# Three start-up stretches of a hybrid encoder layer in another order: filter-tap folds in attention, five products of MLP block 1 among the last norms, the second MLP product's first loads on ScalarE's queue

## The chip, the cores and the metric

The kernel runs on one core of one Trainium2 chip. The metric is the device time of one execution in microseconds (us), lower is better; a run's time is a little longer than the span between its first and last instruction in the trace.

## What is computed

One encoder layer in fp32 for 2048 tokens of width 1024. Cut to what matters here:

```python
a = rms_norm(h, norm1_g)
q, k, v, u = split(a @ w_in)              # 512, 128, 128, 1536 columns
att = block_attention(rope(norm(q)), rope(norm(k)), v)   # 8 heads of 64, 2 key/value heads
hy = hyena_mixer(u, ...)                  # short convolution, two long filters by FFT
mix = concat([rms_norm(att, attn_out_g), rms_norm(hy, hy_out_g)])
h = h + mix @ w_out                       # 1024 x 1024
m = rms_norm(h, norm2_g)
h = h + square(relu(m @ w_mlp_in)) @ w_mlp_out   # 1024 -> 4096 -> 1024
return rms_norm(h, final_g)
```

## The kernel before

Every fp32 product is split into high and low fp32r parts and done as three matmuls (`mm3`, lines 162 to 166: high by high, high by low, low by high). So a left operand is made in two steps: ScalarE casts the high part, VectorE subtracts to get the low part. The stages follow each other: input projection, attention (1238 us at its end) with the projection of u and the filter taps woven in, the transform of the filters and the convolutions, `mix` (the output projection with norm, 1770 to 1895 us), `mlp_in` (to 2525 us) and `mlp_out` (from 2541 us).

**Attention.** A unit of work is 128 queries and one key/value head. Its scores go to TensorE (`peak`, L461; VectorE takes the maxima, L464), then 16 steps of exponentials on ScalarE (L484). GpSimd adds the 16 exponential tiles into `sum` (L489), then `os` (L494), ScalarE copies the weighted values beside it (L505), and GpSimd adds the two halves to `ob` (L507), from which TensorE makes `of` (L513). GpSimd works through its instructions strictly in order. Towards the end of attention the generator `taps_ahead` opens a `Feed`: it loads tiles `x` of the filter taps from memory (L1381, on SP's queue) and folds each into `e` with one addition and one subtraction (L1398, L1399). The engines take turns by `FOLD = gps, vec, gps, gps`; five folds are made ahead, and a tile scheduler, not a hand-written order, decides where they stand between the sums.

**The mix and MLP block 1.** Both MLP products use seven products of half-size operands in place of eight (Strassen's scheme). `mix` walks over 16 token tiles (iteration n = 0 to 15). Per tile: `added` and `squared` (residual, sum of squares), `normed` (m), `turned` (eight transposes into `mt` on TensorE, L776), `taken` (ScalarE copies `mt` with the gain into `sa` or `sb`, L790). Tiles come in pairs; after the second, four subtractions (L802) make the operands of the seven products, and `keep` stores them to `mo_d` by DMAs that GpSimd issues (L799). `sb` has one buffer, so the copies of a tile into it wait until the stores of the pair before have landed. This part is written in program order for TensorE, VectorE, ScalarE and GpSimd (`in_order`). The generator `mlp_in` is stepped from within by `next(mlp)`: it loads blocks of `w_mlp_in` as `w1raw`, and `prepare` makes a left operand `wop` (ScalarE L914, VectorE L915). For product 6, 7, 5 or 3 of a block it first needs the sums `ws` of quarter blocks (`left_sums`, L705 to L708: VectorE in block 0 of the loop, GpSimd later). Those `ws` lie in the pool `mi`, which takes the memory of the pool `mx` of the mix, and is opened only after it. Products are written (block, p); `seq` runs (0,1), (0,2), (0,6), (0,7), (0,5), (1,1), (1,2), (0,3), (1,6) ... by `CYCLE`. Before, (0,1) and (0,2) are made while the last tiles are normed, and everything else after the mix is through.

**The second MLP product.** `mlp_out` runs over steps (p, f). A step loads 512 KB of hidden values `ar` from `H_d` and 256 KB of weights `x`, splits both (`ah` L1090 and L1112, `bh` L1082) and makes 24 matmuls `y`. The first `OLOAD = 3` steps are loaded ahead: the first on ScalarE's queue, the others on SP's, in whose queue the last stores of `H_d` stand before them. Their tiles lie where `mlp_in` had its own, so a load can wait for what was there.

Of the kernel before, what the change touches and what calls it, by code (L numbers as in the profile page):

```python
# [20 lines left out]
P = 128  # L21
# [423 lines left out]
def attention(k, a1, ps, side):  # L445
# [12 lines left out]
    def peak(u, i):  # L458
        b, h = i // G, i % G
        s = ps.get("sc", "sc")  # L460
        nc.tensor.matmul(s[:], u.q[:, h], kt[u.kv, b][0][:], start=True, stop=True)  # L461
        if i == 0:
            u.top = a1.tile([P, G, 4], F32, name="top", bufs=2)
        nc.vector.tensor_reduce(out=u.top[:, h, b:b + 1], in_=s[:], axis=AX.X, op=ALU.max, negate=True)  # L464
        if i == 15:
            low = a1.tile([P, 16], F32, name="low", bufs=2)[:, :G]
            nc.vector.tensor_reduce(out=low, in_=u.top[:], axis=AX.X, op=ALU.min)
            u.diag = a1.tile([P, G, P], F32R, name="diag", bufs=2)
            nc.vector.tensor_mul(out=u.diag[:], in0=k.ident[:].unsqueeze(1).to_broadcast([P, G, P]),
                                 in1=low.unsqueeze(2).to_broadcast([P, G, P]))  # L470
# [6 lines left out]
    def weights(u, j):  # L477
# [10 lines left out]
        elif j < 15:  # L488
            nc.gpsimd.tensor_add(out=u.sum[:], in0=u.p0[:] if j == 1 else u.sum[:], in1=p[:])  # L489
# [228 lines left out]
M_SLOT = {1: 0, 2: 1, 3: 3, 4: 6, 5: 4, 6: 5, 7: 2}  # L718


def mix(k, mo, pool, ps, wo, mlp):
# [5 lines left out]
    k.mh, k.ml = ([mo.tile([P, 4, 4, P], F32R, name=f"m{part}{i}", bufs=1) for i in range(7)] for part in "hl")  # L727
# [28 lines left out]
    def room(u):  # L756
        u.m = mo.tile([P, DM], F32, name="m", tag="raw", bufs=NRAW)
        u.ssq = pool.tile([P, 1], F32, name="r2s", bufs=2)
# [20 lines left out]
    def taken(u):  # L779
# [3 lines left out]
        if s == 0:  # L783
            k.sa = pool.tile([P, 2, 4, P], F32, name="sa", bufs=2)
        else:
            k.sb = pool.tile([P, 5, 4, P], F32, name="sb", bufs=1)
# [4 lines left out]
        if s:  # L791
            op = [k.sa[:, 0], k.sa[:, 1]] + [k.sb[:, j] for j in range(5)]
            b11, b21, b12, b22, t1, t2, t4 = op
            engine = nc.gpsimd if half and i == 3 else nc.vector

# [5 lines left out]
            def sub(out, in0, in1, *js):  # L801
                engine.tensor_sub(out=out, in0=in0, in1=in1)  # L802
# [29 lines left out]
    for n in range(NT):  # L832
# [34 lines left out]
        if n % 2 == 0:  # L867
            add_up(5)
# [4 lines left out]
    for j in range(2):  # L873
        added(old, j)
    squared(old)
    normed(old)
    taken(older)
    add_up(99)
    turned(old)
    taken(old)  # L880
# [6 lines left out]
def mlp_in(k, mo, ps):  # L887
# [3 lines left out]
    raws, sums, ops, blk = {}, {}, {}, {}  # L891
    k.mi = None

# [7 lines left out]

    def prepare(n, p):
# [5 lines left out]
        if p == 6:  # L908
            t = [k.mi.tile([P, 4, P], F32, name=f"ws{i}", bufs=1 + (i == 3))[:] for i in range(4)]
            q = sums[n][0]  # L910
            left_sums(nc.gpsimd if n else nc.vector, *t, q["11"], q["12"], q["21"], q["22"])
            sums[n].update({3: t[3], 5: t[0], 6: t[1], 7: t[2]})
# [14 lines left out]
    def tile(name, bufs):  # L927
        return k.mi.tile([P, 512], F32, name=name, bufs=bufs)
# [34 lines left out]
    for x in seq[:2]:  # L963
        prepare(*x)
        early.append(product(*x))
    yield
    for x in seq[2:LEAD]:
        prepare(*x)
    for i, (n, p) in enumerate(seq):
# [4 lines left out]
        b, g = blk[n], early[i] if i < 2 else product(n, p)  # L974
# [41 lines left out]
def mlp_out(k, pool, ps):  # L1016
# [31 lines left out]
    for name, new in ("wr", raw_w), ("ah", parts_h):  # L1048
# [3 lines left out]
    for name, new in ("x", kept), ("bh", parts_w), ("ar", raw_h):  # L1052
        held[name] = [new()]
# [6 lines left out]
    def load(i):  # L1060
        p, f = steps[i]
        queue = nc.sync if i else nc.scalar
# [95 lines left out]
    nc.sync.dma_start(out=k.gf[:], in_=a["final_g"].unsqueeze(0).to_broadcast([P, DM]))  # L1158
    for i, (p, f) in enumerate(steps):
        if i + OLOAD < len(steps):  # L1160
# [279 lines left out]
def taps_ahead(k, ps):  # L1440
# [4 lines left out]
    yield  # L1445
    yield
    for _ in range(FEED_F[1] - 1):
        k.feed.fold_next()
# [305 lines left out]
def encoder_layer(tc, a):  # L1754
    with ExitStack() as ctx:
# [10 lines left out]
        with sbuf(k, "wa") as k.wa:  # L1766
            with Banks(k, "ps3", {"s": 4}, {"x": 2}) as ps:
# [9 lines left out]
                with sbuf(k, "mo") as mo:  # L1777
                    mlp = mlp_in(k, mo, ps)
                    with sbuf(k, "mx") as mx, in_order(tc):
                        mix(k, mo, mx, ps, k.wo1, mlp)  # L1780
# [22 lines left out]
```

## Time and profile before

| | us |
|---|---|
| median of three runs | 3157.62 |
| lowest, highest | 3154.59, 3162.08 |
| the profiled execution | 3165.88 |
| its span in the trace | 3164.1 |
| TensorE busy in it | 2989.5 |

Read it with TensorE in mind: the span is TensorE's busy time and what lies between. A row of an engine in order of time gives the start, the duration, the instruction, and in brackets the idle time before it with what ended that. A matmul of 512 columns shows 0.39 us at the full clock of 2.4 GHz and 0.63 us at 1.2 GHz, since the rows overlap; matmuls follow each other at 0.23 and 0.43 us.

### The profile page before, as it was taken

To read this page: it belongs to the slowest core of one execution; us is meant where nothing else is said; L and a number is where in the kernel's file an instruction comes from. 1 tells how busy PE (TensorE), PEld (TensorE's weight loads), DVE (VectorE), ACT (ScalarE), POOL (GpSimd) and SP (SyncE) were. 2 spreads that over 40 slices of the span, in tenths; PEclk is the share of its full clock that TensorE was granted. 3 is DMA by queue.
4 is the path that set the end of the run, shared out by engine and by line. 5 is a ranking of instruction groups with operands and counts; after the bars stand their busy time and mean duration, and the time that the engine had idled before them with its cause. 6 is when DMAs were issued, how large, how long until landed. Compare 5 with 4: busy or idle time off the path is not lost.

```text
span 3164.1 us, 40514 instructions
## 1 busy us (share of the span) xinstructions
PE 2989.5 (94%) x13400; PEld 2251.3 (71%) x13400; DVE 2048.8 (65%) x3153; ACT 1423.2 (45%) x2626; POOL 1715.1 (54%) x1399
## 2 busy tenths in 40 slices
PE   8978999999998998999999988999999989999998
PEld 6755666666665666676667766888788778888887
DVE  7987777666665554777465567778877535454455
ACT  7866655555553444444444563333433223223333
POOL 3434777778776876244555326777876635250010
PEclk9988999999998999999999998999999999999999
DMA  7758334324334425776656784445644395333454
GB/s 226 221 155 232 115 125 159 110 95 151 125 107 108 140 80 163 263 248 218 186 172 197 253 290 157 156 154 174 204 158 151 121 316 171 133 115 129 146 181 153
DMA packets 482462, 534.45 MB, mean 169 GB/s; under 512 B 49604, under 2 KB 344004, under 8 KB 475212
## 3 DMA queue, kind: packets, MB, share of 16 engines
q1 hardware_dynamic: 464540, 513.16, 50.4%
q0 software_dynamic: 4480, 14.68, 1.3%
q10 hardware_dynamic: 13232, 4.01, 0.6%
q8 instruction: 107, 1.75, 0.2%
q14 instruction: 103, 0.84, 0.1%
HBM read 326.22 MB, written 198.19 MB: 166 GB/s over the span
## 4 chain that ended last, share of the span: by engine, by line
PE 75%; DVE 5%; DMA 5%; issue 3%; POOL 3%; ACT 2%; SPq 1%; ACTq 0%; POOLq 0%; DVEq 0%
PE o L502 7%; PE y L164 6%; PE y L165 6%; PE y L166 6%; PE g L166 5%; PE g L165 5%; PE g L164 5%; PE st L481 4%; PE X L1435 4%; PE st L482 3%; PE sc L461 3%; PE uo L164 3%; PE uo L165 2%; PE uo L166 2%; PE b L1565 2%
## 5 line engine op out<-in xcount | busy, mean ns | idle before, releaser
L489 POOL TENSOR_TENSOR sum<-sum,p 128x512 f32<-128x512 f32 x416 | 552.9, 1329 | 125.3 <-ACT p L484 98.9
L464 DVE TENSOR_REDUCE top<-sc 128x1 f32<-128x512 f32 x512 | 347.4, 687 | 255.4 <-PE sc L461 252.3
L484 ACT ACTIVATE p<-st 128x512 f32<-128x512 f32 x512 | 303.2, 597 | 317.6 <-PE st L482 299.9
L164 PE MATMUL g<-mh,wop 128*128 128x512 f32 x896 | 350.5, 391 | 17.9 <-ACT wop L914 17.6
L165 PE MATMUL g<-ml,wop 128*128 128x512 f32 x896 | 350.6, 391 | 2.8 <-DVE ml L925 2.8
L166 PE MATMUL g<-mh,wop 128*128 128x512 f32 x896 | 350.4, 391 | 2.4 <-DVE wop L915 2.4
L164 PE MATMUL y<-bh,ah 128*128 128x512 f32 x768 | 299.8, 391 | 15.5 <-ACT bh L1082 15.5
L1091 DVE TENSOR_TENSOR ah<-ar,ah 128x1024 fp32r<-128x1024 f32 x111 | 148.9, 1342 | 235.2 <-ACT ah L1090 232.9
L165 PE MATMUL y<-bh,ah 128*128 128x512 f32 x768 | 299.7, 390 | 0.0
L166 PE MATMUL y<-bh,ah 128*128 128x512 f32 x768 | 299.7, 390 | 0.0
L1090 ACT CAST ah<-ar 128x1024 fp32r<-128x1024 f32 x111 | 117.0, 1054 | 347.8 <-PE y L166 343.0
L502 PE MATMUL o<-p,vt 128*64 128x512 f32 x1024 | 234.9, 598 | 0.0
L461 PE MATMUL sc<-kt,q 128*128 128x512 f32 x512 | 208.0, 410 | 15.0 <-DVE top L464 11.9
L481 PE MATMUL st<-q,kt 128*128 128x512 f32 x512 | 215.0, 420 | 1.6 <-ACT p L484 1.4
L164 PEld LDWEIGHTS g<-mh,wop 128*128 128x128 f32 x896 | 169.2, 189 | 54.2 <-ACT wop L914 18.0
L482 PE MATMUL st<-q,kt 128*128 128x512 f32 x512 | 203.8, 398 | 0.0
L165 PEld LDWEIGHTS g<-ml,wop 128*128 128x128 f32 x896 | 169.0, 189 | 38.9 <-DVE ml L925 3.9
L166 PEld LDWEIGHTS g<-mh,wop 128*128 128x128 f32 x896 | 169.1, 189 | 38.4 <-DVE wop L915 3.5
L914 ACT CAST wop<-ws 128x512 fp32r<-128x512 f32 x128 | 79.1, 621 | 223.5 <-PE g L166 192.1
L164 PEld LDWEIGHTS y<-bh,ah 128*128 128x128 f32 x768 | 144.7, 189 | 46.2 <-ACT bh L1082 15.9
L166 PEld LDWEIGHTS y<-bh,ah 128*128 128x128 f32 x768 | 144.7, 188 | 30.3
L165 PEld LDWEIGHTS y<-bh,ah 128*128 128x128 f32 x768 | 144.7, 188 | 30.2 <-DVE bh L1083 0.2
(306 smaller groups left out, 7054.6 us busy)
## 6 DMA issues: line engine op xcount, KB each, us to landing
ar<-H_d SPq DMA_DIRECT2D x111, 512.0 KB, 3.8
uw<-uw_d SPq DMA_DIRECT2D x36, 1024.0 KB, 5.0
w1raw<-in_w_mlp_in SPq DMA_DIRECT2D x64, 512.0 KB, 4.2
H_d<-r SPq DMA_DIRECT2D x96, 256.0 KB, 2.2
H_d<-s SPq DMA_DIRECT2D x96, 256.0 KB, 2.0
F_d<-F SPq DMA_DIRECT2D x34, 512.0 KB, 3.2
F<-F_d SPq DMA_DIRECT2D x34, 512.0 KB, 4.6
aT<-aT_d SPq DMA_DIRECT2D x32, 512.0 KB, 6.6
```

Of the source, the lines that this page charges most:

```text
L164: mm(out, l_hi, r_hi, start=start, stop=False)
L165: mm(out, l_hi, r_lo, start=False, stop=False)
L166: mm(out, l_lo, r_hi, start=False, stop=stop)
L461: nc.tensor.matmul(s[:], u.q[:, h], kt[u.kv, b][0][:], start=True, stop=True)
L464: nc.vector.tensor_reduce(out=u.top[:, h, b:b + 1], in_=s[:], axis=AX.X, op=ALU.max, negate=True)
L481: nc.tensor.matmul(s[:], lo[:, c], u.q2[:].rearrange("p h t -> p (h t)"), start=True, stop=False)
L482: nc.tensor.matmul(s[:], hi[:, c], u.q[:].rearrange("p h t -> p (h t)"), start=False, stop=True)
L484: nc.scalar.activation(out=p[:], in_=s[:], func=AF.Exp)
L489: nc.gpsimd.tensor_add(out=u.sum[:], in0=u.p0[:] if j == 1 else u.sum[:], in1=p[:])
L502: nc.tensor.matmul(u.o[cols], vt[j // 8][:, j % 8, u.kv], p[:], start=j < 2, stop=j > 13)
L1091: nc.vector.tensor_sub(out=h[:, 1], in0=raw[:], in1=f32(h[:, 0]))
L1435: k.nc.tensor.matmul(d[:, ri], t[:, m], Af[:, 2 * j + at], start=True, stop=True)
```

## The change

It has three parts.

In attention, `taps_ahead` waits one step longer, and each of the five folds is ordered behind the most recent `sum` addition of GpSimd and the most recent maximum of VectorE (`issue_after`). What is loaded and folded is the same.

At the end of the mix, products (0,6), (0,7) and (0,5) join (0,1) and (0,2) among the last tiles' norms: `mlp_in` yields more often and `mix` steps it after each part of the last tile. For that the block 0 sums `ws` lie in the pool `wa` (`lefts`), the last tile's `m` in the mix's own pool, `sb` in a pool `mt` on the other side of the memory, and the operand tiles are allocated in the order in which they are last used. The subtractions of the last pair go from GpSimd to VectorE, and those of the pair before are made one tile earlier. Four tiles that had been allocated at their first use are allocated ahead (`held`).

In `mlp_out`, the loads of all three first steps go on ScalarE's queue, the tiles are allocated in another order, and the load of `gf` (the final gain) moves from before the steps to step 8.

```diff
             u.top = a1.tile([P, G, 4], F32, name="top", bufs=2)
-        nc.vector.tensor_reduce(out=u.top[:, h, b:b + 1], in_=s[:], axis=AX.X, op=ALU.max, negate=True)
+        k.mark_v = nc.vector.tensor_reduce(out=u.top[:, h, b:b + 1], in_=s[:], axis=AX.X, op=ALU.max, negate=True)
...
         elif j < 15:
-            nc.gpsimd.tensor_add(out=u.sum[:], in0=u.p0[:] if j == 1 else u.sum[:], in1=p[:])
+            k.mark = nc.gpsimd.tensor_add(out=u.sum[:], in0=u.p0[:] if j == 1 else u.sum[:], in1=p[:])
...
 M_SLOT = {1: 0, 2: 1, 3: 3, 4: 6, 5: 4, 6: 5, 7: 2}
-def mix(k, mo, pool, ps, wo, mlp):
+LAST_USED = 0, 1, 5, 2, 4, 3, 6
+def mix(k, mo, pool, top, ps, wo, mlp):
...
     nc.scalar.dma_start(out=g2[:], in_=a["norm2_g"][0].rearrange("(d p) -> p d", p=P), allow_slow_non_contiguous=True)
-    k.mh, k.ml = ([mo.tile([P, 4, 4, P], F32R, name=f"m{part}{i}", bufs=1) for i in range(7)] for part in "hl")
+    made = {(part, i): mo.tile([P, 4, 4, P], F32R, name=f"m{part}{i}", bufs=1) for i in LAST_USED for part in "hl"}
+    k.mh, k.ml = ([made[part, i] for i in range(7)] for part in "hl")
...
     def room(u):
-        u.m = mo.tile([P, DM], F32, name="m", tag="raw", bufs=NRAW)
+        own = u.n == NT - 1
+        u.m = (pool if own else mo).tile([P, DM], F32, name="m", tag="h" if own else "raw", bufs=3 if own else NRAW)
...
         else:
-            k.sb = pool.tile([P, 5, 4, P], F32, name="sb", bufs=1)
+            k.sb = top.tile([P, 5, 4, P], F32, name="sb", bufs=1)
...
             b11, b21, b12, b22, t1, t2, t4 = op
-            engine = nc.gpsimd if half and i == 3 else nc.vector
...
             def sub(out, in0, in1, *js):
-                engine.tensor_sub(out=out, in0=in0, in1=in1)
+                nc.vector.tensor_sub(out=out, in0=in0, in1=in1)
...
             added(u, 0)
-        if n % 2 == 0:
+        if n % 2 == 0 or n == NT - 1:
...
         added(old, j)
+    next(mlp)
     squared(old)
+    next(mlp)
     normed(old)
+    next(mlp)
     taken(older)
-    add_up(99)
     turned(old)
+    next(mlp)
...
     NB = 2 * DFF // 256
-    raws, sums, ops, blk = {}, {}, {}, {}
-    k.mi = None
+    raws, sums, ops, blk, held = {}, {}, {}, {}, {}
...
+    def lefts(n):
+        q = sums[n][0]
+        if n:
+            t = [k.mi.tile([P, 4, P], F32, name=f"ws{i}", bufs=1 + (i == 3))[:] for i in range(4)]
+        else:
+            t = [k.wa.tile([P, 4, P], F32, name="ws", tag=tag, bufs=2)[:] for tag in ("mx", "mx", "oh", "ol")]
+        left_sums(nc.gpsimd if n else nc.vector, *t, q["11"], q["12"], q["21"], q["22"])
+        sums[n].update({3: t[3], 5: t[0], 6: t[1], 7: t[2]})
...
             sums[n] = {1: q["11"], 2: q["12"], 4: q["22"], 0: q}
-        if p == 6:
-            t = [k.mi.tile([P, 4, P], F32, name=f"ws{i}", bufs=1 + (i == 3))[:] for i in range(4)]
-            q = sums[n][0]
-            left_sums(nc.gpsimd if n else nc.vector, *t, q["11"], q["12"], q["21"], q["22"])
-            sums[n].update({3: t[3], 5: t[0], 6: t[1], 7: t[2]})
+        if p == 6 and 6 not in sums[n]:
+            lefts(n)
...
     def tile(name, bufs):
-        return k.mi.tile([P, 512], F32, name=name, bufs=bufs)
+        return held.pop(name, None) or k.mi.tile([P, 512], F32, name=name, bufs=bufs)
...
         early.append(product(*x))
+    lefts(0)
...
         prepare(*x)
+        if x is not seq[LEAD - 1]:
+            yield
+    for x in seq[2:LEAD - 1]:
+        early.append(product(*x))
+    yield
+    early.append(product(*seq[LEAD - 1]))
+    yield
+    held.update((name, tile(name, bufs)) for name, bufs in (("sn", 2), ("u2", 1), ("u4", 1), ("r", 4)))
...
             blk[n] = Ctx()
-        b, g = blk[n], early[i] if i < 2 else product(n, p)
+        b, g = blk[n], early[i] if i < LEAD else product(n, p)
...
-    for name, new in ("wr", raw_w), ("ah", parts_h):
+    for name, new in ("ar", raw_h), ("ah", parts_h), ("bh", parts_w), ("x", kept), ("wr", raw_w):
...
         hs[1, t] = pool.tile([P, DM], F32, name="hs1", bufs=8)
-    for name, new in ("x", kept), ("bh", parts_w), ("ar", raw_h):
-        held[name] = [new()]
...
         p, f = steps[i]
-        queue = nc.sync if i else nc.scalar
+        queue = nc.sync if i >= OLOAD else nc.scalar
...
         prepare(i)
-    nc.sync.dma_start(out=k.gf[:], in_=a["final_g"].unsqueeze(0).to_broadcast([P, DM]))
     for i, (p, f) in enumerate(steps):
+        if i == 8:
+            nc.sync.dma_start(out=k.gf[:], in_=a["final_g"].unsqueeze(0).to_broadcast([P, DM]))
...
     k.feed = Feed(k, "tx", k.a["dft_taps"], [k.taps_d[0], k.taps_d[1]], FOLD, FEED_F, fold=False)
-    yield
-    yield
+    for _ in range(3):
+        yield
     for _ in range(FEED_F[1] - 1):
-        k.feed.fold_next()
+        with k.tc.issue_after(k.mark.ins), k.tc.issue_after(k.mark_v.ins):
+            k.feed.fold_next()
...
                     mlp = mlp_in(k, mo, ps)
-                    with sbuf(k, "mx") as mx, in_order(tc):
-                        mix(k, mo, mx, ps, k.wo1, mlp)
+                    with sbuf(k, "mx") as mx, sbuf(k, "mt", side="right") as mt, in_order(tc):
+                        mix(k, mo, mx, mt, ps, k.wo1, mlp)
...
```

Where this moves instructions. First GpSimd in attention, where `ob` of one unit is added; a name's number tells buffers apart, `e` is a folded tile. Before:

```order
L489 TENSOR_TENSOR sum_9511<-p_9509,p_9521 128x512
L1398 TENSOR_TENSOR e_9779<-x_9567 128x4x64
L1399 TENSOR_TENSOR e_9779<-x_9567 128x4x64
L1398 TENSOR_TENSOR e_10006<-x_9571 128x4x64
L1399 TENSOR_TENSOR e_10006<-x_9571 128x4x64
L1398 TENSOR_TENSOR e_10127<-x_9573 128x4x64
L1399 TENSOR_TENSOR e_10127<-x_9573 128x4x64
L1398 TENSOR_TENSOR e_11637<-x_9575 128x4x64
L1399 TENSOR_TENSOR e_11637<-x_9575 128x4x64
L507 TENSOR_TENSOR ob_9540<-os_9496,os_9497 128x512
L489 TENSOR_TENSOR sum_9511<-sum_9511,p_9545 128x512
```

After, from the same `ob` on into the next units:

```order
L489 TENSOR_TENSOR sum<-p 128x512
L507 TENSOR_TENSOR ob<-os 128x512
L489 TENSOR_TENSOR sum<-sum,p 128x512 x6
L1414 TENSOR_TENSOR e<-x 128x4x64
L1415 TENSOR_TENSOR e<-x 128x4x64
L489 TENSOR_TENSOR sum<-sum,p 128x512 x7
L494 TENSOR_TENSOR os<-sum,p 64x512 x2
L489 TENSOR_TENSOR sum<-p 128x512
L507 TENSOR_TENSOR ob<-os 128x512
L489 TENSOR_TENSOR sum<-sum,p 128x512 x4
L1414 TENSOR_TENSOR e<-x 128x4x64
```

The four GpSimd folds stood in one piece ahead of `ob`; now `ob` follows its sums directly and each fold stands between later sums.

Second ScalarE at the end of the mix, from the casts for products (0,1) and (0,2) on; `ws` without a number, and then `w1raw`, are block 0 operands, `sb<-mt` is the last tile's. Before:

```order
L914 CAST wop<-w1raw 128x512 x2
L754 ACTIVATE m,r2s<-h 128x1024
L764 ACTIVATE r2e<-r2y 128x1
L770 ACTIVATE m<-h,r2r 128x512
L790 ACTIVATE sa<-mt,g_15974 128x128 x8
L790 ACTIVATE sb<-mt,g_15974 128x128 x8
L979 COPY sn<-g 128x512
L914 CAST wop<-ws_17264 128x512
L914 CAST wop<-ws_17265 128x512
L914 CAST wop<-ws_17263 128x512
```

After:

```order
L922 CAST wop<-ws 128x512
L767 ACTIVATE r2e<-r2y 128x1
L773 ACTIVATE m<-h,r2r 128x512
L922 CAST wop<-ws 128x512
L793 ACTIVATE sa<-mt,g_15977 128x128 x8
L922 CAST wop<-w1raw 128x512 x2
L922 CAST wop<-ws 128x512
L793 ACTIVATE sb<-mt,g_15977 128x128 x8
L996 COPY sn<-g 128x512
L922 CAST wop<-ws_17343 128x512
```

The casts of block 0's sums stood behind the eight copies into `sb`; now they stand before them, between the steps of the last tile's norm.

Third ScalarE at the start of `mlp_out`, behind the last activations of `mlp_in`. Before:

```order
L947 ACTIVATE r<-r 128x512 x4
L1069 DMA ar<-H_d 128x2x512
L1057 DMA x<-in_w_mlp_out 128x512
L1112 CAST ah<-ar 128x512 x2
L1082 CAST bh<-x 128x512
L1090 CAST ah<-ar 128x1024
L1082 CAST bh<-x 128x512
```

After:

```order
L955 ACTIVATE r<-r 128x512 x4
L1084 DMA ar<-H_d 128x2x512
L1072 DMA x<-in_w_mlp_out 128x512
L1084 DMA ar<-H_d 128x2x512
L1072 DMA x<-in_w_mlp_out 128x512
L1084 DMA ar<-H_d 128x2x512
L1072 DMA x<-in_w_mlp_out 128x512
L1097 CAST bh<-x 128x512
L1127 CAST ah<-ar 128x512 x2
L1105 CAST ah<-ar 128x1024
```

Where one pair of loads stood before the first casts there are three, and the weight's cast `bh` now stands before the hidden values' `ah`.

## Rows read from the trace of the kernel before

**Rows 1.** The page's part 1: busy time and share of the span by engine.
```profile
PE 2989.5 (94%) x13400; PEld 2251.3 (71%) x13400; DVE 2048.8 (65%) x3153; ACT 1423.2 (45%) x2626; POOL 1715.1 (54%) x1399
```

**Rows 2.** Waits of TensorE: engine, line, awaited line, us in total, times, longest us.
```profile
PE g L164 <- ACT wop L914: 17.6, 2, 15.0
PE y L164 <- ACT bh L1082: 15.5, 1, 15.5
PE of L513 <- POOL ob L507: 15.4, 2, 14.7
```

**Rows 3.** Chain of waits, 974 to 1000 us: start us, us, what.
```profile
975.53 13.80 DMA x<-taps_d
```

**Rows 4.** GpSimd in order of time, 974 to 1000 us: start us, us, what, idle before.
```profile
989.36 0.72 POOL L1398 TENSOR_TENSOR e<-x 128x256 f32<-128x256 f32 x1 [12.61 <-DMA x<-taps_d]
...
995.20 1.26 POOL L507 TENSOR_TENSOR ob<-os 128x512 f32<-128x512 f32 x1
```

**Rows 5.** TensorE in order of time, after that wait and at a later sum.
```profile
996.51 1.97 PE L513 MATMUL of<-fold,ob 128*128 128x65 f32 x8 [14.67 <-POOL ob L507]
998.24 0.77 PE L481 MATMUL st<-q,kt 128*128 128x512 f32 x1
...
1003.38 0.39 PE L164 MATMUL uo<-aT,uw 128*128 128x512 f32 x1
...
1083.07 1.00 PE L513 MATMUL of<-fold,ob 128*128 128x65 f32 x8
```

**Rows 6.** GpSimd in order of time, the next two times that ob is added.
```profile
1052.62 1.30 POOL L507 TENSOR_TENSOR ob<-os 128x512 f32<-128x512 f32 x1 [1.56 <-ACT os L505]
...
1080.85 1.29 POOL L507 TENSOR_TENSOR ob<-os 128x512 f32<-128x512 f32 x1 [3.01 <-ACT os L505]
```

**Rows 7.** The page's part 6, DMA issues: count, KB each, median us to landing.
```profile
ar<-H_d SPq DMA_DIRECT2D x111, 512.0 KB, 3.8
uw<-uw_d SPq DMA_DIRECT2D x36, 1024.0 KB, 5.0
```

**Rows 8.** TensorE in order of time, 1844 to 1929 us.
```profile
1844.69 1.94 PE L776 MATMUL mt<-ident,m 128*128 128x128 f32 x8 [4.08 <-DVE m L769]
...
1884.70 1.04 PE L776 MATMUL mt<-ident,m 128*128 128x128 f32 x8
1888.26 0.50 PE L164 MATMUL g<-mh,wop 128*128 128x512 f32 x1 [2.52 <-ACT wop L914]
...
1910.18 0.79 PE L164 MATMUL g<-mh,wop 128*128 128x512 f32 x1 [15.03 <-ACT wop L914]
...
1918.12 0.39 PE L164 MATMUL g<-mh,wop 128*128 128x512 f32 x1
...
1928.35 0.39 PE L164 MATMUL g<-mh,wop 128*128 128x512 f32 x1
```

**Rows 9.** Chain of waits, then ScalarE, VectorE, GpSimd in order of time, 1890 to 1916 us.
```profile
1896.97 6.57 DMA mo_d<-sb
...
1903.69 2.17 ACT L790 ACTIVATE sb<-mt,g 128x128 f32<-128x128 f32 x8 [7.57 <-DMA mo_d<-sb]
...
1894.39 1.29 DVE L802 TENSOR_TENSOR sb<-sb 128x512 f32<-128x512 f32 x2
...
1906.64 2.23 DVE L707 TENSOR_TENSOR ws<-w1raw 128x512 f32<-128x512 f32 x1
...
1914.42 1.65 POOL L707 TENSOR_TENSOR ws<-w1raw 128x512 f32<-128x512 f32 x1 [0.40 <-DVE wop L915]
```

**Rows 10.** ScalarE, its queue, the chain and TensorE, 2522 to 2541 us.
```profile
2526.06 0.63 ACT L947 ACTIVATE r<-r 128x512 f32<-128x512 f32 x1 [2.03 <-DVE r L1005]
2532.17 0.44 ACTq L1069 DMA_DIRECT2D ar<-H_d  x1
...
2532.70 7.37 DMA x<-in_w_mlp_out
...
2540.82 1.22 PE L164 MATMUL y<-bh,ah 128*128 128x512 f32 x2 [15.53 <-ACT bh L1082]
```

## The prediction

> **What bounds the kernel now.** I read the page's busy times first: TensorE works 2989.5 of 3164.1 us [rows 1], so the span is TensorE's work and about 175 us between. The change takes no matmul away; it can only gain where TensorE waits. The list of TensorE's waits, second, shows three that happen once and are about 15 us long [rows 2]: `of` waits for GpSimd's `ob` (14.7), a product of MLP block 1 for ScalarE's `wop` (15.0), the first `y` of the second MLP product for ScalarE's `bh` (15.5). No other wait in the middle of the program comes near. These are the three places that the diff touches, so each was read in the chain of waits and engine by engine in order of time. Together they are 45.2 us, 1.4% of the span.
>
> In attention the chain shows a DMA: a load of filter taps that takes 13.80 us [rows 3]. GpSimd's first fold waits 12.61 us for it, and four folds later, at 995.20, comes `ob` [rows 4], whose own inputs the chain does not name. The wait is one of order, not of need. At the mix's end the chain shows a store of `mo_d` that lands 6.57 us after its start, and only then can ScalarE copy the last tile into `sb`, having been idle 7.57 us [rows 9]; the sums for product (0,6) stand behind that. In front of `mlp_out` ScalarE is through with its last activation at 2526.69, but its first load is issued at 2532.17, and the weight lands 7.37 us after 2532.70 [rows 10].
>
> **Part A, the folds.** Moved away from `ob`, they leave it waiting for its own inputs alone; a later `of` starts 0.93 us after its `ob` ends and has no wait in front [rows 5, 6]. So the 14.67 us go. With them goes a stretch at the low clock: after the wait the eight matmuls of `of` take 1.97 us instead of 1.00, and the 12 matmuls from 998.24 to 1003.38 take 5.14 us [rows 5] instead of 12 x 0.227 = 2.73 (0.227 is the pitch of the 45 matmuls from 1918.12 to 1928.35 [rows 8]). Upper end: 14.67 + 0.97 + 2.41 = 18.05.
>
> What is given back: four folds stay on GpSimd, 5.84 us in all from 989.36 to 995.20 [rows 4], and now stand between sums of the next units. In two such units GpSimd is idle 1.56 and 3.01 us in front of `ob` alone [rows 6], so a fold of 1.46 us is covered unless two fall into one unit; there the second leans on the 3.01. The fifth fold stays on VectorE: its two operations between maxima, at 0.65 us each by the nearest undisturbed row (two subtractions in 1.29), or at worst 2.23 each, as one of VectorE's sums took beside GpSimd's work [rows 9]. If nothing were covered, A would be 18.05 - 5.84 - 4.46 = 7.75. I take 17.5, near the upper end, since the idle time stands in front of the very instruction that matters. Range 8 to 18. The loads of `x` change too: the next ones wait on SP's queue until a fold has freed their tile, and loads of `uw` and of queries stand behind them; that is the rival on the other side, below.
>
> The 2.23 us show that a VectorE operation with two SBUF inputs can take three times its usual time. The Trainium skill (GPSIMD Engine Reference, Key points) says that GpSimd shares its SBUF interfaces with VectorE and that VectorE's instructions with two SBUF inputs contend with it. By that rule the folds, now run beside sums, should cost nearer 4.46 than 1.3 on VectorE, and A would come out at 14 rather than 17.5; the row agrees with the rule, but maxima read PSUM and have one input, so most of VectorE's work there is not of that kind.
>
> **Part B, the mix's end.** Before, from 1884.70: two sets of transposes (1.04 each), products (0,1), (0,2), then the 15.03 us, then from 1910.18 product (0,6), which needs until 1918.12 (7.94 us, because of the low clock and a wait inside) instead of 12 x 0.227 = 2.73, and five more products at 2.73 up to (1,6): 1918.12 + 13.65 = 1931.8 [rows 8]. The same eight products and transposes stand ahead of (1,6) in the changed order, 23.9 us of work; TensorE alone could be there at 1908.6.
>
> It will not be. First, VectorE makes four subtractions of the pair before ahead of the low parts of (0,1): 4 x 0.65 = 2.6 us, so (0,1) starts some 2 us later than 1888.26. Four products follow, 10.9 us, to 1901.4. VectorE and ScalarE now make the sums and casts for (0,6), (0,7), (0,5) between the steps of the last tile's norm, so its `m` comes later; I allow 1.1 us of waiting and 1.04 for the transposes: 1903.6. Then a chain that TensorE does not cover: ScalarE's eight copies into `sb` (2.17 [rows 9], and 0.5 for the start), VectorE's four subtractions (2.6, in place of GpSimd's slower ones), the stores, which land after up to 6.57 us [rows 9] (I take 5.5, since fewer stand in the queue), and only then, since `ws` of block 1 still lies over the mix's memory, two GpSimd sums of 1.65 us and a cast for (1,6), 0.6 by ScalarE's activation of the same shape [rows 10]: 1903.6 + 2.7 + 2.6 + 5.5 + 3.3 + 0.6 = 1918.3, about 1919 with issue. TensorE has four products for that time, to 1914.5; then it waits about 4.5 us. After a wait of 4.08 us eight transposes took 1.94 us instead of 1.04 [rows 8], so this wait costs clock as well; I put 2.4, as at A. Gain: 1931.8 - 1919 - 2.4 = 10.4; I take 10. Ends: 5, if `m` is 5 us later still, and 15, if the stores land early and the wait is too short for the clock to fall.
>
> **Part C, the start of `mlp_out`.** The first pair of loads now goes out behind the last activation: 2526.69 instead of 2532.17, 5.4 us earlier, if what lay in its tiles is long free; the tiles are allocated in another order for that. With the same 7.37 us of landing TensorE starts 5.4 us earlier. With the 3.8 us that such a load takes in the median [rows 7] the bound would be ScalarE's queue: four more loads stand there ahead of the casts, and the last of them wait for the stores of `mlp_in` and for the first pair; I take them as out by 2533, then `bh` and half of `ah`, 128x512 each, at some 0.63 like the activation at 2526.06, and 0.2 to start: 2534.5, 6.3 us earlier than 2540.82 [rows 10]. I take 5.8. Ends: 2, if those four loads hold the casts up by 4 us, and 7. The low clock behind the wait stays: a wait of 9 us remains. `gf` off SP's queue and the other tile orders I cost at nothing: nothing waits there.
>
> A load's 7.37 us are landing, not issue. The Trainium skill (DMA: Bandwidth & Descriptors, "Issuing engines are not separate DMA queues") says that transfers started by different engines run on the same DMA engines and interleave, so that spreading them saves only issue time. By that rule six loads thrown in together slow the first pair down, and C would come to 3 us instead of 5.8; the sum would be 30.5. No row here shows six such loads at once.
>
> **The sum.** 17.5 + 10 + 5.8 = 33.3 us. The profiled execution took 3165.88, so it would take 3132.6; it lies 8.3 us above the median of the runs, 3157.62, and nothing in the three places explains that, so I take the sum off the median: **3124.3 us**. Its own range: all upper ends, 18 + 15 + 7 = 40, give 3117.6; all lower ends, 8 + 5 + 2 = 15, give 3142.6.
>
> **The rivals.** First, B turns one wait into another: the chain over the stores into `ws` of block 1 ends no sooner than before, apart from the early stores. For it: the stores and the overlaid memory stay; against: five products now fill the time. B is then 3 and the time 3157.6 - 26.3 = 3131.3. Second, A gives back its uncovered cost, 7.75 in place of 17.5: 3134.1. For it: a fold pair lies between sums of one unit; against: the idle time in rows 6. Third, C does not do what it says: one of the six loads on ScalarE's queue waits for a store or an earlier load, the casts stand behind it, and TensorE starts as before: 3130.1. Fourth, slower: SP's queue in attention. A load of `x` whose tile is freed only by a fold that now waits for a later sum holds up the loads of `uw` and of queries behind it. It decides when the held load comes later than its use less its landing, 5.0 us [rows 7]; from then TensorE stops at every such fold. Priced at the 13.80 us of the load in rows 3 for each of four GpSimd folds, 55 us, it gives 3157.6 - 33.3 + 55 = 3179. Against it: SP had room between its loads there, and a unit between two `ob` is 28.2 us long [rows 6].
>
> **How the numbers follow.** Chances: forecast 0.63; B lost 0.12; A half given back 0.10; C lost 0.07; several at once, within 6.3 us of the time before, 0.02; SP's queue 0.06. A measurement of this kernel tells about 0.2%, 6.3 us, from no change. The first four are all faster by more: 0.92; same 0.02; slower 0.06. The range takes in all but the last two: from 3114 (3117.6 less the 3 us by which the lowest run lay below the median) to 3143.
>
> **What would show it.** A: no wait of `of` above 3 us, `ob` directly behind `os`, no low clock near 1000 us, no new wait of `uo` or `sc` up to 1090. B: no wait of 15 us; one of 3 to 6 us in front of (1,6), ended by a cast of `ws`; the stores of the last pair landing just before. C: the first `ar` issued on ScalarE's queue by 5 us earlier against the last `g`, and a wait of 9 to 10 us instead of 15.53. I am wrong if TensorE shows new waits in attention after 1030, if the wait at (1,6) is over 8 us, or if later steps of `mlp_out` wait for `ar`.

## The result, and the profile after

The changed kernel takes 3131.47 us in the median (3129.86 to 3133.50, four runs), the kernel before 3158.39 beside it: a ratio of 0.991, 95% interval 0.9897 to 0.9923, so 26.9 us or 0.9% faster. Forecast were 3124.3, range 3114 to 3143, and a gain of 33.3. The direction and the range held, the size was 6 us too large. Two later comparisons of the same two kernels gave 0.9916 (0.9898 to 0.9934) and 0.9904 (0.9891 to 0.9917), 25.9 and 30.7 us between the medians, so the gain is known to some 2 us only: about 28. One execution of part B alone took 3752.47 us at a granted clock of 0.75 and is left out of every number below.

One correction of the part on the change: the order of GpSimd after the change that is printed there begins at the `sum` and `ob` of the next unit, not at the same `ob`; the folds are where the sentence behind it says.

TensorE's list of waits after the change (engine, line, awaited line, us in total, times, longest us):

```profile
PE y L164 <- ACT ah L1127: 12.4, 1, 12.4
...
PE g L164 <- ACT wop L922: 5.4, 2, 4.0
```

Of the three waits of about 15 us in [rows 2], two are gone: `of` no longer waits for `ob`, and the wait of `g` for `wop` has shrunk to 4.0. The third is still there with 12.4 in place of 15.5, and ends now with ScalarE's `ah`. TensorE itself is as busy as before, 2985.5 us against 2989.5 [rows 1]:

```profile
PE 2985.5 (95%) x13400; PEld 2247.5 (72%) x13400; DVE 2047.3 (65%) x3157; ACT 1421.5 (45%) x2626; POOL 1717.1 (55%) x1395
```

**Attention.** GpSimd and then TensorE in order of time, at the `ob` that had waited:

```profile
980.68 1.30 POOL L507 TENSOR_TENSOR ob<-os 128x512 f32<-128x512 f32 x1 [3.40 <-ACT os L505]
...
982.20 1.00 PE L513 MATMUL of<-fold,ob 128*128 128x65 f32 x8
```

`ob` waits for ScalarE's copies alone, and `of` takes its 1.00 us with no wait and no low clock, against 1.97 behind 14.67 in [rows 5]. The folds, further on, in GpSimd's and VectorE's rows:

```profile
1016.12 0.74 POOL L1414 TENSOR_TENSOR e<-x 128x256 f32<-128x256 f32 x1
...
1022.08 7.51 POOL L489 TENSOR_TENSOR sum<-sum,p 128x512 f32<-128x512 f32 x5 [1.51 <-ACT p L484]
...
1041.72 0.74 POOL L1414 TENSOR_TENSOR e<-x 128x256 f32<-128x256 f32 x1
...
1053.60 0.74 POOL L1414 TENSOR_TENSOR e<-x 128x256 f32<-128x256 f32 x1
...
1054.99 0.74 POOL L1414 TENSOR_TENSOR e<-x 128x256 f32<-128x256 f32 x1
...
1063.61 1.27 POOL L507 TENSOR_TENSOR ob<-os 128x512 f32<-128x512 f32 x1
...
1027.54 0.91 DVE L1414 TENSOR_TENSOR e<-x 128x256 f32<-128x256 f32 x1
1028.38 1.50 DVE L1415 TENSOR_TENSOR e<-x 128x256 f32<-128x256 f32 x1
```

The fold at 1016.12 is paid from idle time: 1.51 us are left before the sum at 1022.08. The other three GpSimd folds, from 1041.72, 1053.60 and 1054.99, all fall into one unit, between the `ob` at 1035.11 and that at 1063.61. There the margin is used up: the 3.01 us of [rows 6] in front of `ob` are 0 at 1063.61, but `of` is not late. The fold on VectorE takes 0.91 + 1.50 = 2.41 us, between the 1.3 and the 4.46 that I had put as ends. Both ends were read from rows of 128x512, while a fold's operations are 128x256; in the trace of before this fold took 0.43 + 0.94 us. From 975 to 1200 us TensorE has no wait over 0.2 us.

**The mix's end.** TensorE, then ScalarE, the chain of waits (start us, us, what) and GpSimd:

```profile
1869.80 0.50 PE L164 MATMUL g<-mh,wop 128*128 128x512 f32 x1 [3.98 <-ACT wop L922]
...
1872.42 0.79 PE L166 MATMUL g<-mh,wop 128*128 128x512 f32 x1 [1.89 <-DVE wop L923]
...
1885.38 1.03 PE L779 MATMUL mt<-ident,m 128*128 128x128 f32 x8
...
1898.71 0.50 PE L164 MATMUL g<-mh,wop 128*128 128x512 f32 x1 [1.39 <-ACT wop L922]
...
1899.96 0.50 PE L166 MATMUL g<-mh,wop 128*128 128x512 f32 x1 [0.52 <-DVE wop L923]
...
1867.07 2.17 ACT L793 ACTIVATE sb<-mt,g 128x128 f32<-128x128 f32 x8 [2.96 <-DMA mo_d<-sb]
...
1891.24 3.83 DMA mo_d<-sb
...
1895.49 1.29 POOL L707 TENSOR_TENSOR ws<-w1raw 128x512 f32<-128x512 f32 x1 [2.40 <-DMA mo_d<-sb]
1896.74 1.27 POOL L706 TENSOR_TENSOR ws<-ws,w1raw 128x512 f32<-128x512 f32 x1
```

Four products now stand between 1869.80 and the last tile's transposes at 1885.38, and the wait of 15.03 us in [rows 8] is gone. Before (1,6) at 1898.71 TensorE waits 1.39 us and then 0.52, at the full clock. The chain is the one forecast: a store of `mo_d` lands 3.83 us after its start, GpSimd makes two sums, ScalarE casts. The wait of 3.98 us in front of (0,1) has the same kind of cause: the cast that ends it stands on ScalarE behind the eight copies into `sb` (2.17 us from 1867.07), and these were released by a store of the pair before, 1.2 us after the transposes that they copy had ended.

**The start of `mlp_out`.** ScalarE's casts and its queue, the chain, and TensorE:

```profile
2493.32 0.38 ACTq L1084 DMA_DIRECT2D ar<-H_d  x1
2493.80 0.42 ACTq L1072 DMA_DIRECT2D x<-in_w_mlp_out  x1
2499.89 0.37 ACTq L1084 DMA_DIRECT2D ar<-H_d  x1
2501.22 0.35 ACTq L1072 DMA_DIRECT2D x<-in_w_mlp_out  x1
...
2502.84 0.93 ACTq L1072 DMA_DIRECT2D x<-in_w_mlp_out  x1
2503.81 0.62 ACT L1097 CAST bh<-x 128x512 fp32r<-128x512 f32 x1 [9.87 <-issue]
...
2497.33 3.81 DMA H_d<-r
...
2505.00 0.80 PE L164 MATMUL y<-bh,ah 128*128 128x512 f32 x1 [12.45 <-ACT ah L1127]
```

The first pair of loads now goes out at 2493.32 and 2493.80, beside the last activation; before, 5.5 us behind it [rows 10]. But the first cast, `bh`, starts at 2503.81, directly behind the sixth load on ScalarE's queue. The second pair was not issued before 2499.89 and 2501.22; the chain shows what held its weight, a store of `H_d` that took 3.81 us to land.

Where the time went, by stretches of TensorE's rows. The first runs from the start of one `of` that stands before every change (781.39 in the trace of before) to the first `fs` of the filters' transform, the second to the last `op`, the third to the last `g`, the fourth to the last `y`; all in us, the runs in the order of the experiments below:

| kernel | to first `fs` | to last `op` | to last `g` | to last `y` | wait of first `y` |
|---|---|---|---|---|---|
| before | 455.3 | 647.8 | 640.4 | 627.8 | 15.5 |
| changed | 437.1 | 645.5 | 627.6 | 624.2 | 12.4 |
| A alone | 437.1 | 646.0 | 639.4 | 627.9 | 15.6 |
| B alone | 453.4 | 642.7 | 630.6 | 622.9 | 7.4 |
| C alone | 453.1 | 647.1 | 639.5 | 624.6 | 12.4 |
| before, again | 452.7 | 643.1 | 639.6 | 626.6 | 15.6 |
| changed, again | 437.2 | 645.6 | 627.5 | 623.5 | 11.6 |
| A and B | 437.0 | 645.1 | 630.2 | 622.7 | 7.8 |
| changed, tiles of before | 437.1 | 644.9 | 628.0 | 624.5 | 12.6 |
| two pairs on ScalarE's queue | 437.1 | 649.0 | 627.2 | 622.4 | 10.4 |
| first casts first | 437.0 | 644.6 | 628.1 | 625.0 | 8.8 |
| second `ar` only | 437.0 | 651.5 | 628.0 | 622.2 | 9.3 |
| folds undone | 452.4 | 643.3 | 628.4 | 623.5 | 11.8 |
| changed, third | 437.2 | 648.5 | 627.8 | 624.3 | 12.8 |

### The profile page after: what moved, and what is told of

It is laid out like the page before. It is cut to its first block, busy times and chain, and to the rows that moved or that the text cites. A ratio compares the mean times of both kernels' runs of the same rounds, so it can differ in the third digit from the quotient of the medians.

```text
span 3127.9 us, 40514 instructions
## 1 busy us (share of the span) xinstructions
PE 2985.5 (95%) x13400; PEld 2247.5 (72%) x13400; DVE 2047.3 (65%) x3157; ACT 1421.5 (45%) x2626; POOL 1717.1 (55%) x1395
## 4 chain that ended last, share of the span: by engine, by line
PE 41%; DMA 3%; POOL 2%; issue 2%; ACT 1%; DVE 1%; ACTq 0%; SPq 0%; POOLq 0%; DVEq 0%
PE y L164 7%; PE y L165 7%; PE y L166 7%; PE g L166 5%; PE g L165 5%; PE g L164 5%; PE X L1451 1%; PE b L1582 1%; DMA ml<-sb 1%; PE yo L1647 1%; PE op L166 0%; PE op L164 0%; POOL r L956 0%; PE op L165 0%; ACT sb L793 0%
## 5 line engine op out<-in xcount | busy, mean ns | idle before, releaser
L164 PE MATMUL y<-bh,ah 128*128 128x512 f32 x768 | 300.0, 391 | 12.4 <-ACT ah L1127 12.4
L461 PE MATMUL sc<-kt,q 128*128 128x512 f32 x512 | 208.5, 412 | 13.4 <-DVE top L464 11.6
```

The lines of the kernel that those rows point to most:

```text
L164: mm(out, l_hi, r_hi, start=start, stop=False)
```

## The experiments

The theory after the result: A gives 16 to 18 us, B about 12, C about 3, and the trace of before was of a long execution, so that the traces' difference in span, 36.2 us, is more than the runs'. The rivals: A's wait was an outlier in that one execution; the folds give part back; C's first load is held by landing and not by the queue.

**Part A alone.**

```diff
-        k.feed.fold_next()
+        with k.tc.issue_after(k.mark.ins), k.tc.issue_after(k.mark_v.ins):
+            k.feed.fold_next()
```

> Part A alone on the kernel before. Theory 1 (the traces of before and after, laid side by side, hold for ordinary executions): some 18 us faster, about 3140, the ratio 0.994. Theory 2 (the profiled execution of before had a longer wait of `of` than most executions; it ran 7.5 us above the median): some 9 to 11 us faster, about 3148, ratio 0.9967. Rival (the folds among the sums give part back): the trace shows new TensorE waits of 2 us or more between 1020 and 1090.

Measured: ratio 0.9954 (0.9942 to 0.9966), 14.3 us between the medians. That lies between the two theories; the traces decide below. There is no new wait of 2 us, so the rival of folds that give back falls. The stretch to the first `fs` is 437.1 us, as in the changed kernel.

**Part B alone.**

```diff
+    lefts(0)
     yield
     for x in seq[2:LEAD]:
         prepare(*x)
+        if x is not seq[LEAD - 1]:
+            yield
...
-            k.sb = pool.tile([P, 5, 4, P], F32, name="sb", bufs=1)
+            k.sb = top.tile([P, 5, 4, P], F32, name="sb", bufs=1)
```

> Part B alone. The traces laid side by side give 12.3 us, so about 3146; with the wait at product (1,6) that I forecast, 10. The wait of `of` for `ob` in attention is untouched: theory 1 expects about 14.7 us there again, theory 2 some 6 us.

Measured: 0.9945 (0.9932 to 0.9958), 17.1 us between the medians, more than either number expected. By the stretches 4.5 us of it, which were not expected, are gained in `mlp_out`. ScalarE and TensorE there, in the trace of B alone:

```profile
2508.96 0.63 ACT L955 ACTIVATE r<-r 128x512 f32<-128x512 f32 x1 [2.03 <-DVE r L1022]
2509.10 0.38 ACTq L1086 DMA_DIRECT2D ar<-H_d  x1
...
2513.51 1.14 ACT L1129 CAST ah<-ar 128x512 fp32r<-128x512 f32 x2 [3.92 <-DMA ar<-H_d]
...
2515.59 1.22 PE L164 MATMUL y<-bh,ah 128*128 128x512 f32 x2 [7.39 <-ACT bh L1099]
...
2524.07 0.50 PE L164 MATMUL y<-bh,ah 128*128 128x512 f32 x1 [1.35 <-ACT bh L1099]
2525.41 0.79 PE L165 MATMUL y<-bh,ah 128*128 128x512 f32 x1 [0.84 <-DVE bh L1100]
```

The first `ar` is issued at 2509.10, beside the last activation, without part C: B changes what lies where in the memory, and the tile of that load no longer lies over what the last store of `r` reads and GpSimd's last `s` writes. Before, `s` ended at 2531.38 and the store landed at 2532.07 (its chain row is in the last section), and the load was issued at 2532.17. TensorE waits 7.39 us, less than with B and C together, and gives 1.35 and 0.84 us back at the second step. The wait of `of` in attention is 14.26 us here, so the first theory stands on this point.

**Part C alone.**

```diff
-        queue = nc.sync if i else nc.scalar
+        queue = nc.sync if i >= OLOAD else nc.scalar
```

> Part C alone. The traces give 3.1 us, about 3155, not the 5.8 forecast. If ScalarE's queue with six loads is what holds the first cast (theory), the first `bh` starts right behind the sixth load, as in the changed kernel; the rival, landing, would show the first `x` landing just before `bh`. The wait of `of` in attention is untouched, a further sample.

Measured: 0.9984 (0.9976 to 0.9993), 4.7 us between the medians. ScalarE's queue and casts:

```profile
2520.76 0.38 ACTq L1067 DMA_DIRECT2D ar<-H_d  x1
...
2530.39 0.67 ACTq L1055 DMA_DIRECT2D x<-in_w_mlp_out  x1
2531.11 0.62 ACT L1080 CAST bh<-x 128x512 fp32r<-128x512 f32 x1 [9.78 <-issue]
```

As the theory had it, `bh` stands right behind the sixth load. The wait of `of` was 13.53 us.

**The kernel before, again.**

> The kernel before once more, a null for the comparison: ratio 1.000 within 0.001. Its trace gives another sample of the wait of `of`: 14.7 us by theory 1, some 6 us by theory 2, and a span nearer 3156 than 3164 by theory 2.

Measured: 1.000 (0.9991 to 1.0009), span 3159.3. TensorE at the wait, here and with the folds undone (below):

```profile
999.39 1.97 PE L513 MATMUL of<-fold,ob 128*128 128x65 f32 x8 [13.01 <-POOL ob L507]
```

```profile
992.04 1.97 PE L513 MATMUL of<-fold,ob 128*128 128x65 f32 x8 [12.68 <-POOL ob L507]
```

With 14.67, 14.26, 13.53, 13.01 and 12.68 us in five traces the second theory falls: the wait is there in every execution, though that of the first trace is the longest. The stretch to the first `fs` shows the same: 455.3 us in the first trace, 452.4 to 453.4 in the other four, 437.0 to 437.2 in the nine with part A. A is worth 15.8 us by the four, 18.2 by the first.

**The changed kernel, again.** No edit.

> The changed kernel once more, beside the next three on one chip, as their measure: about 0.991 of before. Its first `y` waits 12 to 13 us, with `bh` directly behind the sixth load on ScalarE's queue.

Measured: 0.9916 (0.9898 to 0.9934); the wait 11.56 us.

**Parts A and B without C.** The edit is the last hunks of the diff undone (queue, tile order, `gf`).

> Parts A and B without part C (queue, tile order and `gf` in the second product as before). Part B alone had the first `y` wait only 7.4 us, since its tiles lie elsewhere. Theory (on top of B, part C holds the first casts up behind six loads and gains nothing): the wait is again 7 to 8 us, two short waits follow at the second step, and the time is equal to the changed kernel or 1 to 2 us better. Rival (C gains 3 us whatever the rest): 3 to 5 us slower than the changed kernel.

Measured: 0.9904 (0.9885 to 0.9923), medians 3127.56 against 3130.76 of the changed kernel beside it. The wait of the first `y` was 7.79 us, two waits of 0.84 and 0.85 followed at the second step: the theory held, and the rival, C's 3 us whatever the rest, fell. The runs don't tell the two kernels apart. By the table C costs 1.3 us in the last stretch and gains 2.6 in the one before. These 2.6 are the edge of the stretch and not part C. The eight transposes ahead of the last `op`, here and in the changed kernel:

```profile
1858.46 1.06 PE L779 MATMUL mt<-ident,m 128*128 128x128 f32 x8 [2.50 <-DVE m L772]
```

```profile
1856.70 1.56 PE L779 MATMUL mt<-ident,m 128*128 128x128 f32 x8 [2.57 <-DVE m L772]
```

In the two kernels that have B without C they run at the full clock, so the last `op` comes sooner, and with it the edge. From the start of these transposes to the last `g` it is 635.4 to 637.0 us in all ten traces with B, 636.4 and 636.8 of them without C, and 647.2 to 648.3 in the four without B.

**Tiles of `mlp_out` in the order of before, all six loads on ScalarE's queue.**

```diff
-    for name, new in ("ar", raw_h), ("ah", parts_h), ("bh", parts_w), ("x", kept), ("wr", raw_w):
+    for name, new in ("wr", raw_w), ("ah", parts_h):
...
+    for name, new in ("x", kept), ("bh", parts_w), ("ar", raw_h):
+        held[name] = [new()]
```

> The changed kernel with the tiles of the second product allocated in the order of before (all six loads stay on ScalarE's queue, `gf` stays at step 8). In this order the second pair of loads waits for nothing that is late; the third waits for the first pair to land. Theory (the second pair's wait for stores of `mlp_in` is what costs in the changed kernel): the wait of the first `y` falls from 12.4 to some 8 to 9 us, 3 to 4 us faster than the changed kernel. Rival (the six loads share the DMA engines and land late whatever they wait for): the wait stays at 11 to 12.5 us.

Measured: 0.9914 (0.99 to 0.9929). This theory fell: the wait was 12.63 us, the second pair was again not issued before 2500.44, 6.2 us behind the first. The time, 3130.55, is that of the changed kernel beside it, 3130.76.

```profile
2494.28 0.42 ACTq L1074 DMA_DIRECT2D x<-in_w_mlp_out  x1
2500.44 0.37 ACTq L1086 DMA_DIRECT2D ar<-H_d  x1
```

So it is not the tile that the load waits for. In the compiled program (not in a trace) the DMAs of SP's and ScalarE's queues signal eight completion semaphores in turn, and each DMA waits until the one eight places before it has landed. The second `ar` waits so for a store of `s`, the second `x` for a store of `r`, which had just been issued; the third pair waits for the first.

**Two pairs on ScalarE's queue.**

```diff
-        queue = nc.sync if i >= OLOAD else nc.scalar
+        queue = nc.sync if i >= 2 else nc.scalar
```

> As the run before, but only the first two pairs on ScalarE's queue and the third on SP's. Nothing on ScalarE's queue then waits for a landing ahead of the first cast: the wait of the first `y` some 7 to 7.5 us, no short waits at the second step, 4 to 6 us faster than the changed kernel, about 3126 where that takes 3131. If landing under load is what counts, no better than the run before.

Measured: 0.9908 (0.9891 to 0.9925). The wait fell to 10.41 us, not to 7; `bh` now starts when the store in front of the second `x` has landed:

```profile
2505.36 0.35 ACTq L1074 DMA_DIRECT2D x<-in_w_mlp_out  x1
2505.80 0.62 ACT L1099 CAST bh<-x 128x512 fp32r<-128x512 f32 x1 [7.83 <-DMA H_d<-r]
```

My expectation that nothing would be waited for was made on the tiles and fell with them. No short wait followed at the second step. The median, 3129.19, is 1.6 us below the changed kernel's beside it, within what the runs can tell; 4 to 6 were expected.

**The first casts ahead of the loads.**

```diff
-    for i in range(OLOAD):
+    load(0)
+    prepare(0)
+    for i in range(1, OLOAD):
         load(i)
-    for i in range(OPREP):
+    for i in range(1, OPREP):
         prepare(i)
```

> The changed kernel with the first pair's casts written ahead of the loads of steps 1 and 2, so that on ScalarE only one of those four loads (the second `ar`) still stands before them. Theory (the first casts wait for ScalarE's queue, not for the data): the first `y` waits 9.5 to 10 us instead of 11.6 to 12.5, some 2 us faster than the changed kernel, if the later loads are still in time. Rival (the data land no sooner): 11.5 us or more.

Measured: 0.9906 (0.9893 to 0.9919), 3130.20 against 3130.24 of the changed kernel beside it. ScalarE, the chain and TensorE come first. Then stand stretches of `mlp_out` with their length, the busy time and count of TensorE, its weight loads, VectorE, ScalarE and GpSimd, and in the last three columns TensorE's clock (a share of full speed), the DMA engines' share and GB/s; below, the same of the changed kernel:

```profile
2498.86 0.37 ACTq L1084 DMA_DIRECT2D ar<-H_d  x1
2499.28 0.62 ACT L1127 CAST ah<-ar 128x512 fp32r<-128x512 f32 x1 [6.22 <-DMA H_d<-s]
...
2500.85 8.39 DMA x<-in_w_mlp_out
...
2500.47 0.80 PE L164 MATMUL y<-bh,ah 128*128 128x512 f32 x1 [8.80 <-ACT bh L1097]
...
2509.94 0.50 PE L164 MATMUL y<-bh,ah 128*128 128x512 f32 x1 [1.54 <-ACT bh L1097]
...
2500.47:2505.47 5.00, 4.99 (x12) 3.65 (x13) 1.35 (x3) 0.47 (x1) 0.00 (x0) 0.57 0.96 355
2505.47:2510.47 5.00, 3.43 (x14) 2.26 (x13) 1.78 (x2) 1.67 (x2) 0.00 (x0) 1.00 1.02 389
2510.47:2520.47 10.00, 9.80 (x36) 7.89 (x37) 5.32 (x7) 4.71 (x6) 0.00 (x0) 0.83 0.92 329
```

```profile
2505.00:2510.00 5.00, 5.00 (x14) 3.84 (x15) 1.36 (x3) 0.97 (x2) 0.00 (x0) 0.59 1.01 388
2510.00:2515.00 5.00, 5.00 (x23) 3.90 (x22) 1.92 (x2) 1.98 (x3) 0.00 (x0) 1.00 1.04 401
2515.00:2525.00 10.00, 10.00 (x46) 8.29 (x45) 5.55 (x7) 5.15 (x8) 0.00 (x0) 1.00 0.92 329
```

The first part of the theory held: the first `y` waits 8.80 us. But the second step waits 1.54 and 0.22, since its weight takes 8.39 us to land, and after that the clock falls once more (0.83 over 10 us, where the changed kernel has 1.00). From the last `g` to the last `y` it is 625.0 us, against 624.3. What came early at the first step was lost at the second.

**Only the first pair and the second `ar` on ScalarE's queue.**

```diff
-        queue = nc.sync if i >= OLOAD else nc.scalar
+        queue = nc.sync if i else nc.scalar
...
-            queue.dma_start(out=t[:].rearrange("p (g e) -> p g e", g=2), in_=k.H_d[p - 1, f].rearrange("g p e -> p g e"))
+            (nc.scalar if i < 2 else queue).dma_start(out=t[:].rearrange("p (g e) -> p g e", g=2), in_=k.H_d[p - 1, f].rearrange("g p e -> p g e"))
```

> Parts A and B, tiles of the second product in the order of before, `gf` at step 8, and on ScalarE's queue the first pair and the second `ar` alone; the second `x` on SP's queue. Theory: the first `y` waits 8.5 to 10 us (one load with a late release ahead of the casts), and the short waits at the second step that the run without part C had are gone: together as good as the best of the others, 2 to 4 us faster than the changed kernel. Rival: the DMA engines are shared and what is gained at the first step is lost at the second, the same time within 1 us.

Measured: 0.9897 (0.9883 to 0.9911), 3129.66. The wait was 9.30 us and 0.81 at the second step; the last stretch, 622.2 us, is the shortest of all, but within 0.6 us of the median the time is the changed kernel's. The rival is nearer. No version of this part beats the changed kernel by more than the runs can tell.

**The folds' order undone in the changed kernel.**

```diff
-        with k.tc.issue_after(k.mark.ins), k.tc.issue_after(k.mark_v.ins):
-            k.feed.fold_next()
+        k.feed.fold_next()
```

> The changed kernel without the ordering of the folds (the additional step of the generator stays; the folds then stand in front of `ob` again, as before). Theory: the wait of `of` is back with 13 to 14.7 us and the low clock behind it, 16 to 18 us slower than the changed kernel: part A is worth the same with B and C as alone. Rival (A was worth less in ordinary executions): 10 us or less.

Measured: 0.9958 (0.9946 to 0.997), 3147.58, so 17.3 us slower than the changed kernel beside it; the wait of 12.68 us is back. The additional step of the generator alone does nothing: the folds stand in front of `ob` as before.

**The changed kernel, a third time.** No edit.

> The changed kernel on the same chip as the three others: 0.991 of before; its spread is the measure of what can be told apart.

Measured: 0.9904 (0.9891 to 0.9917), 3130.24.

## Why the prediction was right, and by how much it was off

**What bounds the kernel** was read rightly: the gain lies at TensorE's three waits of 15 us, and TensorE's busy time is the same within 4 us.

**Part A, 17.5 us:** right in its mechanism, and 1 to 2 us high. Undoing it in the changed kernel costs 17.3 us in the medians, adding it alone gains 14.3; the stretch in the traces says 15.8 by four executions and 18.2 by the one that I worked from. The low clock went with the wait. The folds were covered as argued, with no margin left in the unit that got three. The VectorE fold's 2.41 us bear out the direction of the rule cited from the Trainium skill (GPSIMD Engine Reference, Key points), that two-input work on VectorE contends with GpSimd, but not the 4.46 us that I had worked out by it, and TensorE did not wait for it.

**Part B, 10 us:** about right in sum, and part of that is luck, since wrong terms of opposite sign met. The third stretch is 12.1 us shorter (639.7, the mean of the four traces without B, to 627.6), 11.6 when read from the transposes, and the 4.5 us in `mlp_out` were not forecast at all. The wait at (1,6) came out at 1.9 us in place of 4.5, and without the 2.4 of low clock, because the stores landed in 3.83 us, where I took 5.5, and GpSimd's sums took 1.29 and 1.27, where I took 1.65 (the row that I read them from stood beside VectorE's work). What I undercounted stands at the other end: (0,1) waits 3.98 and 1.89 us for its operand, at the low clock until 1877.7, where I had allowed 2 us for VectorE's four subtractions. The longer of the two waits is for ScalarE, whose cast stands behind the copies into `sb` and these behind a store; that term was missing.

**Part C, 5.8 us:** this step failed. The first loads did go out early, 0.8 us behind the end of the last `g` in place of 6.9, but I took ScalarE's queue as free by 2533, 0.9 us after the landing of the `r` store, which is 7.7 us behind the last `g`. It was free 11.2 us behind it (2503.77 against 2492.55), because the store took 3.81 us to land in place of some 2, and the fifth and sixth loads took 2.2 us to issue, from 2501.61 to 2503.77. I had taken tiles not yet free as what a load waits for, and stores and the first pair for the last loads only. Tiles held the first `ar` of the kernel before; in the changed kernel the second pair already is held, in either tile order, by stores ahead of it in the rotation of semaphores. By the stretches C alone gains 2.8 us (627.4 to 624.6), and the fourth stretch is 3.4 us shorter with all three parts. B alone shortens it by 4.5: I treated B and C as independent, and B already removes what held the first load. On top of B, C gained nothing that the runs can tell (3127.56 without it, 3130.76 with it). The parts measured alone come to 14.3 + 17.1 + 4.7 = 36.1 us, together to 28.

Behind that a second bound is likely. In the first 10 us of `mlp_out` the DMA engines are busy throughout in both kernels compared above (share 0.96 to 1.04, 355 to 401 GB/s). Whichever queue the loads take and whatever stands first, the six kernels that have B, with C left out or altered, and the four traces with both as they are need 622.2 to 625.0 us from the last `g` to the last `y`. That the DMA engines set this is argued and not shown: in the kernel before, which needs 627.8, their share over the same 10 us is already 0.94 and 0.90. The page of the Trainium skill cited in the prediction (DMA: Bandwidth & Descriptors, "Issuing engines are not separate DMA queues") says that transfers started by different engines run on the same DMA engines and interleave. The weight that takes 8.39 us to land beside the others agrees with it, and C alone came out near the 3 us worked out under it, partly by luck: what held the casts first was ScalarE's queue, which from 2494.2 to 2501.2 issued one load and otherwise waited for stores.

**The sum.** Mis-sized were C by about 3 us and the trace that I worked from. The profiled execution ran 7.5 us above the median, and I took none of that off the three parts; 2.4 us of it stood in A's stretch. A by four traces, 15.8, B 12.1 and the last stretch 3.4 make 31.3, the runs say about 28. What takes back the other 3 us isn't settled: the convolution stretch is 1.9 us longer in the mean of the nine traces with part A (646.7) than in the five without (644.8), but both groups spread over 5 us and more. TensorE's waits for folded tiles `e` in that stretch are 8.5 to 10.8 us in the nine and 6.0 to 10.3 in the five, so the later folds may have a part in it; no run separates them.

**The rivals.** The first did not come, though its mechanism, the stores in front of `ws`, is there with 1.9 us. The second did not come. The third came in part: the casts do stand behind loads that wait for stores, at the price of 2.4 us and not of all 5.8. The fourth, SP's queue in attention, left no wait of TensorE up to 1200 us.

## What to carry to other kernels

Where the wait for a single instruction came from its place in a queue, moving what stood in front was worth the whole wait and the low clock behind it, since the work found idle time elsewhere; that part could be forecast to some 3 us from rows. Loads put on a compute engine's queue stand in front of its arithmetic: ask of each what it waits for in turn, semaphores of earlier stores among it, before counting its early issue as gain. And edits that change the memory's layout are not independent: two parts that free the same load are not paid twice.

## What had not been expected of the hardware

What follows a wait of some 4 us can run at either clock: `g` behind 3.98 us started at the full one and fell to the low one behind the next wait, of 1.89 us, while after 1.39 and 0.52 us at (1,6) it stayed full, and the eight transposes behind 4.08 us took 1.94 us [rows 8], at the low one. Nor do waits of like length tell: behind 2.57 us the transposes above took 1.56, behind 2.50 only 1.06. And the store of `r` took longer to land where loads were in flight beside it; the chain of before and of C alone:

```profile
2530.07 2.00 DMA H_d<-r
```

```profile
2524.71 3.92 DMA H_d<-r
```

That is 2.00 us against 3.92, and 3.81 in the changed kernel.
